# A two-layer trunk on one core: the first MLP with eight plain block products, its activations kept in SBUF

## The chip, the core and the metric

The kernel runs on one core of a Trainium2 chip. The metric is the device time of one execution in microseconds (us). The kernel before takes 2790.23 us, the median of three runs from 2789.31 to 2793.01 us.

The engines are named as the profile names them: PE is TensorE (matmuls), PEld its weight loads, DVE is VectorE, ACT is ScalarE, POOL is GpSimd, SP is SyncE, which here only issues DMAs.

## What is computed

The reference is a trunk of two layers over a sequence of 1024 tokens, 1024 channels wide. Layer 0 mixes tokens by retention, layer 1 by an S5 state-space layer. Each mixer is followed by an MLP with a causal convolution of width 3 on its gate. Every sub-layer is normed, and shifted, scaled and gated by the conditioning vector:

```python
def conv_ffn(h, w_up, conv_w, conv_b, w_down):
    val, gate = jnp.split(h @ w_up, 2, axis=-1)          # 1024 -> 2 x 2816
    gate = lax.conv_general_dilated(gate, conv_w, ...) + conv_b   # depthwise, 3 taps
    return (jax.nn.silu(gate) * val) @ w_down            # 2816 -> 1024

for i in range(DEPTH):                                   # 0: retention, 1: S5
    h = rms_norm(x) * (1.0 + sc1) + sh1
    x = x + g1 * mixer(h)
    h = rms_norm(x) * (1.0 + sc2) + sh2
    x = x + g2 * conv_ffn(h, ...)
return rms_norm(x) * final_norm_g
```

All of it is float32. The changed part is `conv_ffn` of layer 0.

## The kernel before

**Products.** Channels lie on the 128 partitions, tokens on the free axis, in two halves of 512 tokens (`hf`), which is one PSUM bank. A float32 product is made from split operands: each operand is a high part and a low part, and `mm3` issues three matmuls for each 128 x 128 weight block (high x high, high x low, low x high), at lines 765 to 767. A weight tile of 128 x 1024 is loaded raw (`wr`), and split by ScalarE (`whi`) and VectorE (`wlo`) into a ring of five. The class `Stream` (`W`) holds all weights of the program in one list, loads up to three raw tiles ahead, and splits the next one when the code asks for it (`get`) or passes a call of `pump`. The order of instructions is simply the order in which the Python code records them: each engine runs its instructions in that order and waits by semaphores.

**The MLP before.** `ffn` serves both layers. For one tile `ff` of 128 of the 2816 channels it makes gate and value of all tokens, a product of a 2 x 2 block matrix (gate and value by the two halves of the input channels) with another (the input halves by the token halves), from seven block products (`pair`) in place of eight. Each block product is 4 x 3 matmuls. Three things come with it: sums of weight blocks, made by GpSimd (`add_up`); sums of blocks of the normed activations, made once (`steps_s`, tiles `hs`); and sums of results: a bank gets one product, VectorE adds it into `u` or `E`, and then the same bank takes a second product on top (`b1`, `b3` and `b4` in `pair`). The convolved, gated result goes to DRAM (`store`, `ff_d`), since the slots of SBUF are full, and is read back and split for the down projection (`f_load`, `f_split`, tiles `fr`, `fh`, `fl`). Also x itself is stored before the MLP and read back for the down projection (`x_in`). The down projection runs over six groups of three or four tiles, after all up products.

**The background job.** While the first MLP runs, `s5_weights` makes the matrices of the S5 layer: 8 tiles with two rounds each, so 16 rounds. It is a Python generator. The MLP's code calls `bg` at fixed places, and each call records the job's next step; a bare `yield` ends a step, and `yield True` ends it and the call. A round is: products of table entries on GpSimd (`outer`), four transposes on TensorE (line 1392), angles and sines on GpSimd, VectorE and ScalarE, a second set of products, and four or eight small matmuls on TensorE (line 1414, the kernel products). After a tile's second round a small result goes to DRAM and comes back by eight loads (line 1431) in another layout, ScalarE reorders it (line 1439), and it is stored (`t_d`). The next tile starts behind that.

**Lead-ins.** Norms run in steps as well: `nrm.step` records the next one between groups of matmuls. `steps` makes the normed activations as pairs `hh`, `hl` for plain products (retention and S5 layers); `steps_s` makes the block sums for `pair`.

Of the kernel before, what the change touches and what calls it, by code (L numbers as in the profile page):

```python
# [18 lines left out]
P = 128  # L19
T = 1024  # L20
# [61 lines left out]
def trunk_kernel(ctx: ExitStack, tc: tile.TileContext, x, c, pos, ada_w, ada_b, ret_w_in, ret_w_out,  # L82
# [50 lines left out]
    def hsl(h):  # L133
        return slice(h * HW, (h + 1) * HW)
# [8 lines left out]
    def weight_list():  # L143
# [22 lines left out]
        yield from ffn_list(1)  # L166

    LEADS = 5
    GROUPS = ((0, 4), (4, 8), (8, 12), (12, 15), (15, 18), (18, 22))
# [3 lines left out]
    def ffn_list(l):  # L173
        wu, wd = ffn_w_up[l], ffn_w_down[l]
        for ff in range(LEADS):
            yield ("uv", l, ff), cols8(wu, ff * P), 8
        for ff in range(NFF):
            yield ("up", l, ff), (cols8(wu, FF + ff * P), cols8(wu, ff * P)), Q5 if ff < LEADS else Q7
        for ff in range(NFF):
            yield ("dn", l, ff), wd[ff * P:(ff + 1) * P, :].rearrange("p (o n) -> p o n", o=1), 1  # L180

    class Stream:
# [121 lines left out]
        def extra(self, i):  # L304
            key = self.items[i][0]
            return key[0] == "dn" and (key[2] % 8 > 4 and key[2] < GROUPS[-1][0] or key[2] in (1, 2))

# [1034 lines left out]
    def s5_weights():  # L1342
# [13 lines left out]
        nxt = load(0)  # L1356
        for _ in range(5):
            yield
        for j in range(8):
# [5 lines left out]
            for hf in range(2):  # L1365
# [67 lines left out]
            yield True  # L1433
            yield True
            yield True
            yield True
            yield True
            yield True
# [3 lines left out]
            yield True  # L1442
            yield True
        drop(sev)
# [121 lines left out]
    for b in range(1, HEADS):  # L1566
# [30 lines left out]
    ff_d = [tc.dram_tile((NFF, P, T), F32, name=f"ff{l}_d") for l in range(2)]  # L1597

    def ffn(l, finish, SB, behind=None):
        nonlocal xs  # L1600
        f_d = ff_d[l]
        e = t_p.tile([P, 1280], F32, tag="tA", name="E")
# [338 lines left out]

    ffn(0, finish0, SB, s5_weights())

# [356 lines left out]
```

## Time and profile before

| what | us |
|---|---|
| median of three runs | 2790.23 |
| the profiled execution | 2790.11 |
| its span, first to last instruction | 2788.3 |
| TensorE busy | 2628.9 |
| VectorE busy | 1763.3 |
| GpSimd busy | 1055.6 |
| ScalarE busy | 932.5 |

The span is one execution, as the hardware profiler saw it. A matmul of 512 columns is shown with a length of 0.39 us, while the next starts 0.227 us after it: matmuls overlap, so the busy time of TensorE is a union, and its pitch has to be read from starts. The stages of the program lie in the span like this, by the first matmul that reads a stage's tiles: retention up to 917 us; first MLP 917 to 1715 us, the down projection's matmuls from 1446 us; S5 layer with its GLU from 1715 to 2067 us; second MLP from 2067 us, its down projection from 2522 us.

### The profile page before, as it was taken

Reading aid. Unit: us, or ns where it says so; the run is one execution under the profiler, and the core shown is the slowest. Engines: PE = TensorE matmul, PEld = TensorE weight load, DVE = VectorE, ACT = ScalarE, POOL = GpSimd, SP = SyncE. Lnnn points to the kernel's source line nnn. Section 1 sums busy time; section 2 is a strip of 40 time slices with the busy share of each in tenths; the row PEclk is TensorE's granted clock in tenths of the full one; section 3 lists DMA queues with packets and bytes.
Section 4 is the critical chain, followed back from the end, with each engine's and each line's share of the span. In section 5 each row is a group of like instructions: output and inputs, shape, how many; then the busy total and the mean of one; then the engine's idle time right before and its main releaser. Section 6 shows DMA issues by size and latency. Waiting matters only on the chain.

```text
span 2788.3 us, 33464 instructions
## 1 busy us (share of the span) xinstructions
PE 2628.9 (94%) x12777; PEld 2199.2 (79%) x12777; DVE 1763.3 (63%) x2347; ACT 932.5 (33%) x1486; POOL 1055.6 (38%) x817
## 2 busy tenths in 40 slices
PE   6999999999999888999989999999998999999998
PEld 5798888888888676777777877888876788888887
DVE  8664664746765787777776654674248876666454
ACT  5332131221322634444433323322144444343112
POOL 5455676765101544655523333221124422310004
PEclk7999999999999999999999999999999999999999
DMA  7644344343532223333345433795221322225211
GB/s 241 169 129 137 121 135 145 117 158 94 168 115 69 91 93 106 119 108 119 113 176 183 137 127 129 248 301 184 75 83 61 106 83 84 83 86 207 101 53 61
DMA packets 319756, 356.59 MB, mean 128 GB/s; under 512 B 39372, under 2 KB 261100, under 8 KB 319596
## 3 DMA queue, kind: packets, MB, share of 16 engines
q1 hardware_dynamic: 278316, 276.17, 31.7%
q10 hardware_dynamic: 41280, 78.28, 7.6%
q8 instruction: 101, 1.65, 0.2%
q14 instruction: 59, 0.48, 0.1%
HBM read 266.64 MB, written 86.15 MB: 127 GB/s over the span
## 4 chain that ended last, share of the span: by engine, by line
PE 64%; DVE 18%; ACT 6%; issue 4%; DMA 4%; POOL 2%; SPq 0%; ACTq 0%; DVEq 0%; POOLq 0%
PE bk L765 20%; PE bk L767 19%; PE bk L766 19%; DVE t L1639 1%; DVE t L1638 1%; DVE whi L335 1%; DVE E L1210 1%; DVE wlo L335 1%; PE bk L1077 1%; PE bk L1075 1%; PE bk L1076 1%; DVE t L1210 1%; DVE sev L1396 1%; POOL ar L128 1%; DMA U<-u_d 1%
## 5 line engine op out<-in xcount | busy, mean ns | idle before, releaser
L765 PE MATMUL bk<-hs,whi 128*128 128x512 f32 x656 | 268.4, 409 | 44.7 <-DVE E L1210 41.2
L1473 DVE SCALAR_TENSOR_TENSOR x<-bk,mods,x 128x512 f32<-128x512 f32 x224 | 184.6, 832 | 192.5 <-PE bk L767 192.4
L766 PE MATMUL bk<-hs,whi 128*128 128x512 f32 x656 | 265.5, 405 | 6.4 <-DVE hs L657 4.3
L322 DVE TENSOR_TENSOR wlo<-wr,whi 128x1024 fp32r<-128x1024 f32 x126 | 179.7, 1430 | 138.4 <-ACT whi L321 138.4
L765 PE MATMUL bk<-hh,whi 128*128 128x512 f32 x640 | 255.7, 400 | 8.3 <-DVE x L1473 4.1
L767 PE MATMUL bk<-hs,wlo 128*128 128x512 f32 x656 | 260.2, 397 | 0.0
L766 PE MATMUL bk<-hl,whi 128*128 128x512 f32 x640 | 253.4, 396 | 3.0 <-POOL hl L128 1.7
L765 PE MATMUL bk<-hs,wlo 128*128 128x512 f32 x576 | 229.4, 398 | 26.0 <-DVE E L1210 26.0
L767 PE MATMUL bk<-hh,wlo 128*128 128x512 f32 x640 | 252.4, 394 | 0.2 <-DVE wlo L322 0.2
L767 PE MATMUL bk<-hs,whi 128*128 128x512 f32 x576 | 231.0, 401 | 0.0
L766 PE MATMUL bk<-hs,wlo 128*128 128x512 f32 x576 | 227.1, 394 | 0.0
L321 ACT ACTIVATE whi<-wr 128x1024 fp32r<-128x1024 f32 x126 | 131.5, 1056 | 284.6 <-PE bk L766 226.1
L765 PEld LDWEIGHTS bk<-hs,whi 128*128 128x128 f32 x656 | 128.7, 196 | 78.2 <-issue 28.1
L765 PE MATMUL bk<-fh,whi 128*128 128x512 f32 (+1 forms) x480 | 183.2, 382 | 5.3 <-ACT nat L2229 3.7
L767 PE MATMUL bk<-fh,wlo 128*128 128x512 f32 (+1 forms) x480 | 181.0, 377 | 0.0
L766 PE MATMUL bk<-fl,whi 128*128 128x512 f32 (+1 forms) x480 | 180.8, 377 | 0.0
L457 POOL TENSOR_TENSOR aacc<-aacc,ar 128x1024 f32<-128x1024 f32 x70 | 172.4, 2463 | 5.8
L128 POOL TENSOR_TENSOR nacc<-nacc,ar 128x512 f32<-128x512 f32 x36 | 46.6, 1294 | 322.1 <-ACT ar L575 321.9
L766 PEld LDWEIGHTS bk<-hs,whi 128*128 128x128 f32 x656 | 129.4, 197 | 34.8 <-DVE hs L657 5.0
L765 PEld LDWEIGHTS bk<-hs,wlo 128*128 128x128 f32 x576 | 110.2, 191 | 53.9 <-ACT wlo L334 12.5
L765 PEld LDWEIGHTS bk<-hh,whi 128*128 128x128 f32 x640 | 122.3, 191 | 35.4 <-ACT hh L611 4.5
L128 POOL TENSOR_TENSOR ar<-sp 128x512 f32<-128x512 f32 (+1 forms) x64 | 83.2, 1314 | 175.8 <-ACT sev L1402 81.8
(375 smaller groups left out, 6706.1 us busy)
## 6 DMA issues: line engine op xcount, KB each, us to landing
ar<-in_ada_w SPq DMA_DIRECT2D x80, 512.0 KB, 4.4
wr<-in_ffn_w_up SPq DMA_DIRECT2D x74, 512.0 KB, 3.8
wr<-in_ret_w_in SPq DMA_DIRECT2D x48, 512.0 KB, 3.8
ff_d<-t ACTq DMA_DIRECT2D x44, 512.0 KB, 2.8
wr<-in_ffn_w_down SPq DMA_DIRECT2D x44, 512.0 KB, 4.2
fr<-ff_d SPq DMA_DIRECT2D x44, 512.0 KB, 5.8
x_d<-x ACTq DMA_DIRECT2D x24, 512.0 KB, 3.1
x<-x_d SPq DMA_DIRECT2D x24, 512.0 KB, 7.2
```

Of the source, the lines that this page charges most:

```text
L128: GP.tensor_tensor(out=out, in0=in0, in1=in1, op=op)
L321: A.activation(out=hi, in_=r, func=AF.Copy)
L322: low = lambda: V.tensor_tensor(out=lo, in0=r, in1=f(hi), op=ALU.subtract)
L335: V.tensor_tensor(out=lo, in0=src, in1=f(hi), op=ALU.subtract)
L457: eng.tensor_tensor(out=acc, in0=acc, in1=raw, op=ALU.add)
L765: PE.matmul(bk, lhsT=lh, rhs=rh, start=first, stop=False, skip_group_check=skip)
L766: PE.matmul(bk, lhsT=lh, rhs=rl, start=False, stop=False, skip_group_check=skip)
L767: PE.matmul(bk, lhsT=ll, rhs=rh, start=False, stop=last, skip_group_check=skip)
L1075: PE.matmul(o, lhsT=hh, rhs=wh[:, k % 4, :], start=(k == 0), stop=False)
L1076: PE.matmul(o, lhsT=hh, rhs=wl[:, k % 4, :], start=False, stop=False)
L1210: V.tensor_tensor(out=o, in0=a, in1=b, op=op)
L1473: V.scalar_tensor_tensor(out=dst, in0=bk, scalar=g, in1=src, op0=ALU.mult, op1=ALU.add)
```

## The change

The first MLP gets a function of its own, `ffn_plain`; the second still calls `ffn`. In `ffn_plain` gate and value of a tile are plain products over the eight blocks of 128 input channels, for each half of the tokens: 24 matmuls into one bank, which is read once. ScalarE copies the gate to a tile `E` (now two of them, in turn), VectorE convolves it and multiplies it by the value's bank, and ScalarE and VectorE split the result at once into `fh` and `fl`, which stay in SBUF. The loop goes over 11 blocks of two tiles: up products of block b + 1, then the down projection of block b, added to x in its place; the last two blocks' down projection is `finish0`, as before with four tiles. The weight list is put in that order. x is neither stored before the MLP nor read back. The background job gets other places for its steps: one in the middle of each up product (`mid=bg`, after the fifth block), one behind it, and one after each m of the down projection; its own `yield`s are changed with it.

```diff
-        yield from ffn_list(0)
+        yield from plain_list(0)
...
+    def plain_list(l):
+        wu, wd = ffn_w_up[l], ffn_w_down[l]
+        for b in range(NB + 1):
+            if b < NB:
+                for ff in (2 * b, 2 * b + 1):
+                    yield ("ug", l, ff), cols8(wu, FF + ff * P), 8
+                    yield ("uv", l, ff), cols8(wu, ff * P), 8
...
+            for ff in dn:
+                yield ("dn", l, ff), wd[ff * P:(ff + 1) * P, :].rearrange("p (o n) -> p o n", o=1), 1
...
                 outer(8, O_RR, O_RI, O_Y1, O_Y2, True)
+                yield
+                yield
...
-                yield True
-                yield True
-                yield True
+                yield
                 bk = bank(6)
...
                 outer(9, O_AR, O_AI, O_Q1, O_Q2, False)
-                yield True
-                yield True
-                yield True
+                yield
+                yield
+                yield
...
-            SB = Blocks()
+            hT = []
...
-                    if hf:
-                        A.dma_start(out=x_d[m], in_=xs[m])
...
-                nrm.start_s(hf, xs, 0, 3, SB, 6, 7)
+                nrm.start(hf, xs, 0, 3, hT, 6, 7)
...
+    def ffn_plain(l, finish):
+        UB = DB = RA
...
+        def up_mm(w, hf):
+            bk = UB()
+            gemm(bk, w, hT, hf, sel=chalf, mid=bg)
+            return bk
+
+        def gate_out(bk, ff, hf):
+            e = E[ff % 2]
+            b3 = as_sel(bk, chalf)
+            A.activation(out=e[:, 2:10, hf * 64:(hf + 1) * 64], in_=b3, func=AF.Copy)
+            n = 64 - hf
+            A.activation(out=e[:, 0:2, hf * 64 + 1:hf * 64 + 1 + n], in_=b3[:, 6:8, 0:n], func=AF.Copy)
+
+        def val_out(bk, ff, hf):
...
+            V.tensor_scalar(out=a3, in0=e[:, 2:10, cs], scalar1=w2_, scalar2=None, op0=ALU.mult)
+            V.scalar_tensor_tensor(out=a3, in0=e[:, 1:9, cs], scalar=w1_, in1=a3, op0=ALU.mult, op1=ALU.add)
+            V.scalar_tensor_tensor(out=a3, in0=e[:, 0:8, cs], scalar=w0_, in1=a3, op0=ALU.mult, op1=ALU.add)
+            A.activation(out=s_, in_=a, func=AF.Silu, bias=cb)
+            V.tensor_tensor(out=s_, in0=s_, in1=bk, op=ALU.mult)
...
+            A.activation(out=hi[:, hsl(hf)], in_=s_, func=AF.Copy)
+            V.tensor_tensor(out=lo[:, hsl(hf)], in0=s_, in1=f(hi[:, hsl(hf)]), op=ALU.subtract)
+
+        def up(b):
+            for ff in (2 * b, 2 * b + 1):
+                wg = W.get(("ug", l, ff))
+                for hf in range(2):
+                    gate_out(up_mm(wg, hf), ff, hf)
+                    tick()
+                wv = W.get(("uv", l, ff))
+                for hf in range(2):
+                    val_out(up_mm(wv, hf), ff, hf)
+                    tick()
+
+        def lead():
...
+            for hf in range(2):
+                for grp in ((0, 1, 2, 3),) if hf == 0 else ((0, 1), (2, 3)):
+                    bks = [UB() for _ in grp]
...
+                    gemm_group(bks, [ws[i] for i in grp], hT, hf, chalf, step)
...
+        lead()
+        for b in range(NB - 2):
+            up(b + 1)
+            ffs = (2 * b, 2 * b + 1)
+            ws = W.get(("dn", l, ffs[0]), 2)
+            for m in range(8):
+                for hf in range(2):
+                    bk = down_mm(ws, ffs, m, hf)
+                    v = chalf(xs[m], hf)
+                    xadd(v, as_sel(bk, chalf), mod(l, 5, m), v)
+                tick()
+            for ff in ffs:
+                drop(*acts.pop(ff))
+        up(NB - 1)
+        bg_drain()
...
-    ffn(0, finish0, SB, s5_weights())
+    bgq.append(s5_weights())
+    ffn_plain(0, finish0)
```

The order of the instructions shows it on VectorE, at the end of a tile's products. Before, in the middle of a `pair`: `tu` is the running sum u, `bk` a bank, `E` the gate to be convolved, `t_7741` its convolution, and the rows of line 335 split weight blocks, among them sums (`sq`).

```order
L1210 TENSOR_TENSOR tu<-tu,bk 128x512
L335 TENSOR_TENSOR whi<-wr,whi 128x512
L1210 TENSOR_TENSOR E<-tu,bk 128x8x64
L335 TENSOR_TENSOR wlo<-wr,wlo 128x512
L1210 TENSOR_TENSOR E<-E,bk 128x8x64
L335 TENSOR_TENSOR whi<-wr,whi 128x512
L1210 TENSOR_TENSOR E<-tu,bk 128x8x64
L1638 SCALAR_TENSOR_TENSOR t_7741<-E,prm,t_7741 128x512
```

Now, from the last value half of a block into the down projection: `t_7740` is the convolution, `t_7741` its silu and then the product with the value's bank, `fl` the low part of the activation, and line 1486 (1473 before) adds a down product to x.

```order
L1638 TENSOR_SCALAR t_7740<-E,prm 128x512
L1639 SCALAR_TENSOR_TENSOR t_7740<-E,prm,t_7740 128x512
L1640 SCALAR_TENSOR_TENSOR t_7740<-E,prm,t_7740 128x512
L1642 TENSOR_TENSOR t_7741<-t_7741,bk 128x512
L1647 TENSOR_TENSOR fl<-t_7741,fh 128x512
L1486 SCALAR_TENSOR_TENSOR x_6527<-bk,mods,x_6527 128x8x64 x2
L339 TENSOR_TENSOR wlo<-wr,whi 128x1024
L1486 SCALAR_TENSOR_TENSOR x_6566<-bk,mods,x_6566 128x8x64 x2
```

The four reads of banks that build u and E are gone, and the additions to x stand directly behind a tile's activation.

On GpSimd, before, inside one round of the background job: `ar` and `sev` are its tiles, `wr`, `wrx` and `sq` the sums of weight blocks.

```order
L128 TENSOR_TENSOR ar<-sp 128x576 x2
L128 TENSOR_TENSOR ar<-ar 128x576
L128 TENSOR_TENSOR wr<-wr,sq 128x512
L128 TENSOR_TENSOR ar<-ar,db 16x2x16 x2
L128 TENSOR_TENSOR ar<-sp 128x4x8x16 x2
L128 TENSOR_TENSOR ar<-ar 128x512
L128 TENSOR_TENSOR sev<-sp,cst 128x512
L1385 TENSOR_SCALAR ar<-sev 128x512
L1386 TENSOR_SCALAR ar<-ar 128x512
L128 TENSOR_TENSOR sq<-wrx 128x512
```

Now, at the same place of a round (lines 1403 and 1404 are 1385 and 1386 before):

```order
L128 TENSOR_TENSOR ar<-sp 128x576 x2
L128 TENSOR_TENSOR ar<-ar 128x576
L128 TENSOR_TENSOR ar<-ar,db 16x2x16 x2
L128 TENSOR_TENSOR ar<-sp 128x4x8x16 x2
L128 TENSOR_TENSOR ar<-ar 128x512
L128 TENSOR_TENSOR sev<-sp,cst 128x512
L1403 TENSOR_SCALAR ar<-sev 128x512
L1404 TENSOR_SCALAR ar<-ar 128x512
```

The sums of weight blocks have left GpSimd's queue; the background job has it to itself. In TensorE's order, some 72 matmuls of the MLP now stand between the transposes of a round and its kernel product, some 48 between that and the second round's transposes, and 108 to 111 between a tile's last kernel product and the next tile's first transposes. From the S5 layer on, all engines have the instructions of before in the order of before.

## Rows read from the trace of the kernel before

**Rows 1.** The page: span, and busy time of each engine.

```profile
span 2788.3 us, 33464 instructions
PE 2628.9 (94%) x12777; PEld 2199.2 (79%) x12777; DVE 1763.3 (63%) x2347; ACT 932.5 (33%) x1486; POOL 1055.6 (38%) x817
```

**Rows 2.** By stretch, first MLP cut in two: length, busy per engine, clock, DMA share, GB/s.

```profile
917.00:1477.00 560.00, 493.84 (x2092) 395.48 (x2092) 425.86 (x505) 251.23 (x425) 280.96 (x221) 0.94 0.35 115
1477.00:1715.00 238.00, 231.19 (x1038) 187.99 (x1037) 136.11 (x158) 77.18 (x92) 87.29 (x81) 0.99 0.40 139
```

**Rows 3.** TensorE's waits, 917 to 1715 us: in total, times, longest.

```profile
PE bk L765 <- DVE E L1210: 50.4, 15, 9.8
PE bk L1414 <- POOL ar L128: 12.5, 6, 3.1
PE bk L1392 <- POOL ar L128: 4.0, 2, 3.3
PE bk L766 <- POOL E L1604: 2.0, 1, 2.0
...
```

**Rows 4.** In order of time, TensorE: start, duration, line, operation, tiles.

```profile
1559.73 0.39 PE L767 MATMUL bk<-fh,wlo 128*128 128x512 f32 x1
...
1563.13 0.39 PE L767 MATMUL bk<-fh,wlo 128*128 128x512 f32 x1
...
1736.63 0.39 PE L767 MATMUL bk<-hh,wlo 128*128 128x512 f32 x1
...
1738.89 0.39 PE L765 MATMUL bk<-hh,whi 128*128 128x512 f32 x1
```

**Rows 5.** Groups by line, TensorE, 917 to 1715 us: count, busy, mean ns, idle before.

```profile
L1414 PE MATMUL bk<-ar,sp 128*16 128x128 f32 x128 | 17.6, 283 | 12.5 <-POOL ar L128 12.5
L1392 PE MATMUL bk<-cst,ar 128*128 128x128 f32 x64 | 9.9, 279 | 4.0 <-POOL ar L128 4.0
```

**Rows 6.** TensorE in order of time, and the stretch 1089 to 1099 us.

```profile
1093.63 0.77 PE L765 MATMUL bk<-hs,whi 128*128 128x512 f32 x1 [9.82 <-DVE E L1210]
...
1089.00:1099.00 10.00, 5.37 (x12) 3.84 (x12) 6.97 (x9) 4.41 (x8) 3.34 (x2) 0.50 0.21 83
```

**Rows 7.** Groups by line, VectorE, 917 to 1715 us.

```profile
L1473 DVE SCALAR_TENSOR_TENSOR x<-bk,mods,x 128x512 f32<-128x512 f32 x96 | 70.9, 753 | 66.0 <-PE bk L767 65.9
L335 DVE TENSOR_TENSOR whi<-wr,whi 128x512 fp32r<-128x512 f32 x48 | 45.7, 953 | 27.4 <-ACT whi L334 27.4
L1638 DVE SCALAR_TENSOR_TENSOR t<-E,prm,t 128x512 f32<-128x512 f32 x44 | 45.5, 1034 | 16.4 <-ACT E L1628 16.4
L1639 DVE SCALAR_TENSOR_TENSOR t<-E,prm,t 128x512 f32<-128x512 f32 x44 | 42.2, 959 | 1.6
...
L322 DVE TENSOR_TENSOR wlo<-wr,whi 128x1024 fp32r<-128x1024 f32 x16 | 21.6, 1354 | 3.1 <-ACT whi L321 3.1
...
L798 DVE TENSOR_SCALAR sev<-sev 128x512 f32<-128x512 f32 x16 | 8.6, 539 | 0.5
```

**Rows 8.** TensorE in order of time, lead-in of the S5 layer.

```profile
1722.77 0.77 PE L765 MATMUL bk<-hh,whi 128*128 128x512 f32 x1 [4.08 <-DVE x L1473]
```

**Rows 9.** One passage of the background job: TensorE, SyncE's queue, ScalarE, TensorE.

```profile
1594.17 1.05 PE L1414 MATMUL bk<-ar,sp 128*16 128x128 f32 x8
...
1600.05 5.04 SPq L1431 DMA_DIRECT2D ar<-ks_d  x8
...
1613.40 2.22 ACT L1439 ACTIVATE ar<-ar 128x1024 f32<-128x1024 f32 x1
...
1621.25 0.89 PE L1392 MATMUL bk<-cst,ar 128*128 128x128 f32 x4 [3.33 <-POOL ar L128]
```

**Rows 10.** VectorE and GpSimd in order of time, 1169 to 1174 us.

```profile
1169.77 1.66 DVE L1639 SCALAR_TENSOR_TENSOR t<-E,prm,t 128x512 f32<-128x512 f32 x1
...
1173.16 0.75 DVE L1639 SCALAR_TENSOR_TENSOR t<-E,prm,t 128x512 f32<-128x512 f32 x1
...
1169.24 1.64 POOL L128 TENSOR_TENSOR sq<-sq,wr 128x512 f32<-128x512 f32 x1
```

More of the change, by code (lines that the diff above doesn't have):

```diff
@@ L180, in ffn_list @@
             yield ("dn", l, ff), wd[ff * P:(ff + 1) * P, :].rearrange("p (o n) -> p o n", o=1), 1
+    def plain_list(l):
[5 more added lines that the diff above has]
+                    yield ("uv", l, ff), cols8(wu, ff * P), 8
+            if b == NB:
+                dn = range(2 * NB - 4, 2 * NB)
+            elif 0 < b < NB - 1:
+                dn = range(2 * b - 2, 2 * b)
+            else:
+                dn = ()
+            for ff in dn:
+                yield ("dn", l, ff), wd[ff * P:(ff + 1) * P, :].rearrange("p (o n) -> p o n", o=1), 1
     class Stream:
@@ L305, in extra @@
             key = self.items[i][0]
-            return key[0] == "dn" and (key[2] % 8 > 4 and key[2] < GROUPS[-1][0] or key[2] in (1, 2))
+            return key[:2] == ("dn", 1) and (key[2] % 8 > 4 and key[2] < GROUPS[-1][0] or key[2] in (1, 2))
         def split(self, later=None):
@@ L1356, in s5_weights @@
         nxt = load(0)
-        for _ in range(5):
-            yield
+        yield
         for j in range(8):
@@ L1432, in s5_weights @@
                              in_=ks_d[j * 8:(j + 1) * 8, :, P - GI * t:2 * P - GI * t].rearrange("g i w -> i g w"))
[L1433 to L1438, printed above, removed]
+            yield
+            yield
+            yield
+            yield
             A.activation(out=tb.rearrange("p (g j t) -> p g t j", g=8, t=8),
@@ L1591, in trunk_kernel, with step, down_mm, down_group @@
                         nrm.behind(m)
-                nrm.start_s(hf, xs, 0, 3, SB, 6, 7)
+                nrm.start(hf, xs, 0, 3, hT, 6, 7)
     for a_, b_ in act:
         drop(a_, b_)
-    ff_d = [tc.dram_tile((NFF, P, T), F32, name=f"ff{l}_d") for l in range(2)]
+    def ffn_plain(l, finish):
+        UB = DB = RA
+        E = []
+        for tag in ("tA", "tD"):
+            e = t_p.tile([P, 1280], F32, tag=tag, name="E")
+            e3 = e.rearrange("p (t c) -> p t c", c=P)
+            GP.memset(e3[:, 0:2, 0:1], 0.0)
+            E.append(e3)
+        t1 = t_p.tile([P, 2, HW], F32, tag="tB", name="t1")
+        t2 = t_p.tile([P, 2, HW], F32, tag="tC", name="t2")
+        acts = {}
+        def up_mm(w, hf):
[9 more added lines that the diff above has]
+        def val_out(bk, ff, hf):
+            w0_, w1_, w2_, cb = convp(l, ff)
+            e = E[ff % 2]
+            cs = slice(hf * 64, (hf + 1) * 64)
+            a, s_ = t1[:, hf, :], t2[:, hf, :]
+            a3 = as_sel(a, chalf)
+            V.tensor_scalar(out=a3, in0=e[:, 2:10, cs], scalar1=w2_, scalar2=None, op0=ALU.mult)
[3 more added lines that the diff above has]
+            V.tensor_tensor(out=s_, in0=s_, in1=bk, op=ALU.mult)
+            if ff not in acts:
+                acts[ff] = (take(F32R, "fh"), take(F32R, "fl"))
+            hi, lo = acts[ff]
+            A.activation(out=hi[:, hsl(hf)], in_=s_, func=AF.Copy)
[11 more added lines that the diff above has]
+        def lead():
+            ws, late = [], {}
+            for i in range(4):
+                ws.append(W.get(("uv" if i % 2 else "ug", l, i // 2), more=(i > 0)))
+                W.pump()
+            for hf in range(2):
+                for grp in ((0, 1, 2, 3),) if hf == 0 else ((0, 1), (2, 3)):
+                    bks = [UB() for _ in grp]
+                    def step(k):
+                        if hf == 0:
+                            nrm.lead(k)
+                        else:
+                            nrm.step()
+                            if k in late:
+                                late.pop(k)()
+                    gemm_group(bks, [ws[i] for i in grp], hT, hf, chalf, step)
+                    for i, bk in zip(grp, bks):
+                        run = partial(val_out if i % 2 else gate_out, bk, i // 2, hf)
+                        if hf:
+                            run()
+                            W.done()
+                            tick()
+                        else:
+                            late[(0, 4, 1, 6)[i]] = run
+        def down_mm(ws, ffs, m, hf):
+            bk = DB()
+            n = len(ffs)
+            for i, ff in enumerate(ffs):
+                wh, wl = ws[i]
+                mm3(bk, wh[:, 0, m * P:(m + 1) * P], wl[:, 0, m * P:(m + 1) * P],
+                    acts[ff][0][:, hsl(hf)], acts[ff][1][:, hsl(hf)], i == 0, i == n - 1)
+            return bk
+        lead()
[8 more added lines that the diff above has]
+                    xadd(v, as_sel(bk, chalf), mod(l, 5, m), v)
+                tick()
+            for ff in ffs:
+                drop(*acts.pop(ff))
+        up(NB - 1)
+        bg_drain()
+        for p_, q_ in hT:
+            drop(p_, q_)
+        ffs = tuple(range(NFF - 4, NFF))
+        ws = W.get(("dn", l, ffs[0]), 4)
+        def down_group(ms, hf):
+            bks = {m: DB() for m in ms}
+            for i, ff in enumerate(ffs):
+                wh, wl = ws[i]
+                for m in ms:
+                    mm3(bks[m], wh[:, 0, m * P:(m + 1) * P], wl[:, 0, m * P:(m + 1) * P],
+                        acts[ff][0][:, hsl(hf)], acts[ff][1][:, hsl(hf)], i == 0, i == 3)
+                if i < 1:
+                    nrm.step(1)
+                if i:
+                    W.done()
+                    W.pump()
+                if i == 3:
+                    nrm.step(2)
+            W.done()
+            return bks
+        def down_part(m, c0, nc):
+            bk = DB()
+            sel = lambda t: t[:, hsl(c0 // 64)].rearrange("p (t c) -> p t c", t=8)[:, :, c0 % 64:c0 % 64 + nc]
+            o = bk[:, 0:8 * nc].rearrange("p (t c) -> p t c", t=8)
+            for i, ff in enumerate(ffs):
+                wh, wl = ws[i]
+                mm3(o, wh[:, 0, m * P:(m + 1) * P], wl[:, 0, m * P:(m + 1) * P],
+                    sel(acts[ff][0]), sel(acts[ff][1]), i == 0, i == 3)
+            return o
+        finish(down_part, down_group)
+        for ff in ffs:
+            drop(*acts.pop(ff))
```

8 lines of the change are left out of this document (5 added, 3 removed).

## The prediction

> **What bounds the kernel now.** I read the page's busy times first, then the stretch of the first MLP cut in two, then TensorE's waits in it, and last the rows from which prices come. TensorE is busy for 2628.9 of 2788.3 us [rows 1]; no other engine comes over 63%. So the time is TensorE's instructions at their pitch, plus the stretches in which it stands still or runs at half clock. The profiled execution took 2790.1 us, 1.8 us more than its span, and the median of the runs is 2790.2 us; the sum below is made against 2790.1.
>
> The first MLP runs from 917 to 1715 us. In its first 560 us (the block products, and the first groups of the down projection) TensorE is busy for 493.8 us and the granted clock averages 0.94; in the other 238 us, all of it down projection, 231.2 us and 0.99 [rows 2]. The waits tell why the two differ: 50.4 us in 15 places stand before a product whose releaser is a VectorE addition into E, line 1210 [rows 3]. That is the chain of the seven products: a bank may take its second product only once VectorE has read the first. Another 12.5 and 4.0 us stand before the small matmuls of the background job that prepares the S5 layer's weights, and wait for GpSimd; what is left is 5.7 us, most of it in the lead-in of the MLP. All nine rows of that view sum to 72.6 us; the four largest are shown. A long wait costs twice: after 9.8 us of idling TensorE works at a granted clock of 0.50, the 1.2 GHz level, for these 10 us [rows 6]. The share of clock lost is 0.06 x 560 + 0.01 x 238 = 36 us.
>
> A check that nothing large is missed: matmuls start every 0.2267 us (15 steps from 1559.73 to 1563.13) in the down projection, and 10 steps from 1736.63 to 1738.89 give 0.226 us for a product that reads half of the normed activations with stride, as the new code will [rows 4]. The MLP has 22 x 7 x 4 x 3 = 1848 up and 22 x 16 x 3 = 1056 down matmuls: 2904 x 0.2267 = 658.3 us. The background's small matmuls take 17.6 + 9.9 = 27.5 us [rows 5]. 658.3 + 27.5 + 72.6 + 36 = 794.4 us of 798.
>
> **The change part by part.**
>
> *TensorE's work.* A gate and value tile now takes eight plain block products in place of seven: 22 x 2 x 2 x 8 x 3 = 2112 matmuls, 264 more. 264 x 0.2267 = +59.8 us, all on the path, since TensorE is what the kernel waits for. The Trainium skill (TensorE: Matmul & The Clock Gate, Back-to-back issue gap) gives 131 ns for such a matmul in a sustained stream, and about 216 ns for one by itself; 264 of them would be 35 or 57 us. The rows have 227 ns in every dense stretch, so the trace disagrees with the first and is 5% above the second.
>
> *The waits of the seven products.* In the new code a bank is filled by 24 matmuls in a row and read once afterwards; no product waits for VectorE between them. Six banks rotate: a bank comes back six products, 6 x 24 x 0.2267 = 33 us, later. VectorE's work on a value half is one scalar multiply, two multiply-adds, the multiply by the bank and the low part. The first is new; I bound it by 0.54 us (line 798) and 0.96 us (line 1639); with 1.03 + 0.96, 0.75 (an instruction that reads a bank, line 1473) and 0.95 us the half costs 4.2 to 4.7 us, where two products take 10.9 us [rows 7]. So the 50.4 us go. What is late next is the background job, below.
>
> *VectorE as a whole.* 44 halves x 4.4 = 194, 66 weight tiles x 1.354 = 89, 160 additions to x at 0.753 = 120 us: 403 us, and about 16 x 5 x 1.0 = 80 us for the background, in 750 us of TensorE work. Before it was 425.9 + 136.1 = 562 us [rows 2, 7]. It has become lighter, mainly as the splitting of block sums and the split on the way back from DRAM are gone. GpSimd loses all its block sums. This counts for VectorE too: one and the same multiply-add takes 1.66 us when it starts during a GpSimd addition and 0.75 us when none runs [rows 10]. The Trainium skill (SBUF — State Buffer, Who interferes with whom) has this as a lock: a VectorE instruction with two SBUF inputs and a GpSimd instruction that reads SBUF exclude each other. The trace agrees.
>
> *DRAM traffic.* 22 stores of activations, 22 loads, and the 8 stores and 8 loads of x around the MLP go. TensorE waits for none of them in [rows 3], so I cost them at nothing; SyncE's queue keeps the weight loads and the background's alone. The up projection's weights are the same bytes, and one weight tile lasts two products, 10.9 us; with three raw and five split buffers a late load is hidden, and would cost its own lateness if not.
>
> *The background job.* It is still 16 rounds with 64 + 128 small matmuls: 27.5 us, unchanged. Its steps are now spaced by half a product, 2.7 us, and in TensorE's order some 72 matmuls (16.3 us) stand between the transposes and the kernel product of a round. GpSimd's three additions there, at about 1.64 us each [rows 10], take 5 us, so most of the 12.5 us should go. The tight place is from one tile's last kernel product to the next tile's first transposes: 108 matmuls or a few more, 24.5 us. Before, one such passage began at 1594.2 us and the transposes came at 1621.25 us after 3.33 us of waiting, 27.1 us in all; in between stand the eight loads from 1600.05 us (5.04 us of issuing) and ScalarE's copy at 1613.40 us [rows 9]. A load of stored activations that is gone now ran between the two. So seven passages wait 0 to 2.6 us each: 0 to 18 us. For all of the background the bounds are 0 and today's 16.5 us plus the lost clock. I take 6 us.
>
> *The lead-in.* The MLP now begins as the S5 layer does, with four products side by side while the norm's second half is made. That lead-in has one wait of 4.08 us [rows 8]; the present one of the MLP has most of the 5.7 us above. Bounds 0 and 8; I take 4 us.
>
> *Lost clock.* 36 us were lost for 72.6 us of waits, 0.5 us for each. 10 us of waits left make 15 us with the clock.
>
> *The sum.* The MLP: 798 - 72.6 - 36 + 59.8 + 15 = 764 us, a gain of 33.8 us: 2790.1 - 33.8 = 2756 us. From the S5 layer on, the engines' instructions are the same as before in the same order, so I cost the rest at nothing.
>
> **The rivals.**
>
> *No wait is left.* Every wait in [rows 3] goes: 72.6 + 36 - 59.8 = 48.8 us gained, 2741 us. For it: the second half of the MLP, with its plain groups, waits for nothing but the background. Against: seven passages with next to no slack. If a matmul could go at the page's 131 ns it would be 2716 us; nothing in [rows 4] speaks for it, and I give it one in a hundred, inside this case.
>
> *The background keeps its waits.* The 16.5 us stay, with 8 us of clock, and the lead-in doubles its 6 us: gain 48.8 - 24.7 - 12 = 12 us, 2778 us. For it: the same chain through ScalarE, GpSimd and DRAM, with fewer steps of patience written between its parts. Against: GpSimd does nothing else now.
>
> *VectorE holds up the down groups (slower).* A down group has 16 half products of 1.36 us, 21.8 us in all, and comes after every second tile, while VectorE still finishes a value half. It has 16 x 0.753 = 12.0 us of additions, up to three weight tiles (4.1 us), a half round of the background (5 us) and 1.7 us left over: 22.8 us at worst, with six banks (8 us) to lean on. If GpSimd's additions stretch these as in [rows 10], it passes 25.7 us, and the 3.9 us more in each of ten groups eat the gain; from there on it is slower. At 28 us the groups cost 62 us with the lost clock neglected: about 2818 us. Against: the second half of the MLP runs such groups with the same job beside them, VectorE 57% busy (136.1 of 238 us), and TensorE waits for no addition to x there [rows 2, 3].
>
> *Nothing gained.* Waits of 33 us (with half as much clock) remain in places that I don't see: 2790 us.
>
> **How the numbers follow.** The forecast, 2756 us with a range of its own of 2745 to 2771, has 0.66. No wait left: 0.11. The background's waits: 0.11. Nothing gained: 0.05. VectorE holds up the groups: 0.07. What a measurement of this kernel can tell from no change is about 0.2%, 5.6 us, so faster has 0.66 + 0.11 + 0.11 = 0.88, same 0.05, slower 0.07. The range from 2740 to 2780 us takes in the first three cases but for their ends and leaves out some 15 in 100.
>
> **What would show it.** TensorE's matmuls of the first MLP go to 2112 + 1056 at 0.227 us; no wait for VectorE's additions into E is left in the first MLP; the MLP lasts about 764 us; the granted clock there is over 0.97; waits before the transposes (line 1392 before) number up to seven and stay under 3 us; the second MLP keeps its own. I am wrong if TensorE waits for additions to x in the down groups, if single waits of over 3 us at the value products keep the clock at half, or if the rest of the span changes by over 5 us.

## The result and the profile after

The changed kernel takes 2743.3 us (median of 4 runs, 2740.0 to 2746.8), the kernel before 2790.1 on the same chip: a ratio of 0.9831 with a 95% interval of 0.9814 to 0.9848, 47 us faster. The forecast was 2756 us, with a range from 2740 to 2780.

First the page of the changed kernel, which answers to [rows 1]:

```profile
span 2740.5 us, 33365 instructions
PE 2652.0 (97%) x13041; PEld 2228.7 (81%) x13041; DVE 1651.2 (60%) x2248; ACT 856.9 (31%) x1348; POOL 908.8 (33%) x724
```

TensorE has 264 instructions more (13041 for 12777) and is busy for 23 us longer, and still the span is 47.8 us shorter: the rest was standing still and half clock. The first MLP, cut at the same 1477 us as in [rows 2] (stretch, length, busy time of PE, PEld, DVE, ACT, POOL with counts, clock, DMA share, GB/s):

```profile
917.00:1477.00 560.00, 551.24 (x2497) 448.88 (x2496) 350.74 (x432) 194.90 (x290) 184.57 (x178) 1.00 0.29 92
1477.00:1672.00 195.00, 195.00 (x876) 160.94 (x876) 97.61 (x127) 55.20 (x84) 32.10 (x30) 1.00 0.22 72
```

TensorE is busy for 551 of the first 560 us, where it was 494, at a clock of 1.00, where it was 0.94. Its waits in the same stretch, which answer to [rows 3] (what was waited for; us in total, times, longest):

```profile
PE bk L782 <- DVE t L1642: 3.5, 2, 2.5
PE bk L1408 <- POOL ar L128: 2.0, 3, 1.0
PE bk L783 <- DVE hl L637: 1.6, 1, 1.6
PE bk L783 <- POOL hl L128: 0.8, 1, 0.8
PE bk L1430 <- POOL ar L128: 0.7, 1, 0.7
```

8.6 us are left of 72.6, and no row names E. (Lines 1408 and 1430 are 1392 and 1414 of before.) The table shows where the span went. A stage runs from its first matmul to the next stage's first; "gaps" is the sum of TensorE's idle times over 0.3 us, "clock" half of the time at a granted clock of 0.50.

| stage | before | gaps, clock | after | gaps, clock |
|---|---|---|---|---|
| ahead of the first MLP | 918.2 | | 917.8 | |
| first MLP | 797.1 | 72.4, 37.5 | 759.5 | 8.6, 0 |
| S5 layer | 351.7 | 8.8, 3.4 | 349.4 | 6.4, 1.7 |
| second MLP, up | 455.1 | 22.7, 10.2 | 454.5 | 22.8, 10.2 |
| its down projection, final norm | 266.2 | 7.7, 1.4 | 259.4 | 2.2, 1.7 |

The first MLP gained 37.6 us. Another 9.1 came from the S5 layer and the last stage, which compute what they did before. The last stage's waits show it best. Before:

```profile
PE bk L765 <- ACT nat L2229: 3.7, 3, 1.4
PE bk L2223 <- DVE xn L1473: 1.6, 2, 0.8
PE bk L765 <- DVE nat L2232: 1.5, 2, 1.0
PE bk L2214 <- DVE facc L2252: 0.9, 1, 0.9
```

And after, the same view:

```profile
PE bk L2364 <- DVE facc L2402: 0.9, 1, 0.9
PE bk L2373 <- DVE xn L1486: 0.7, 1, 0.7
PE bk L782 <- DVE nat L2382: 0.5, 1, 0.5
```

A product of the down projection no longer waits for ScalarE to finish `nat`, the transposed output. These two have nothing to do with each other but a PSUM bank.

### The profile page after: what moved, and what is told of

It is laid out like the page before. It is cut to its first block, busy times and chain, and to the rows that moved or that the text cites. A ratio compares the mean times of both kernels' runs of the same rounds, so it can differ in the third digit from the quotient of the medians.

```text
span 2740.5 us, 33365 instructions
## 1 busy us (share of the span) xinstructions
PE 2652.0 (97%) x13041; PEld 2228.7 (81%) x13041; DVE 1651.2 (60%) x2248; ACT 856.9 (31%) x1348; POOL 908.8 (33%) x724
## 4 chain that ended last, share of the span: by engine, by line
PE 75%; DVE 13%; ACT 4%; DMA 3%; issue 2%; POOL 2%; SPq 0%; ACTq 0%; DVEq 0%; POOLq 0%
PE bk L782 23%; PE bk L784 23%; PE bk L783 23%; PE bk L1094 1%; PE bk L1092 1%; PE bk L1093 1%; DMA W<-w_d 1%; DVE wlo L339 1%; POOL ar L128 1%; ACT whi L338 1%; DVE stf L1167 1%; PE bk L2150 1%; DVE bacc L476 1%; PE bk L1188 1%; DVE gve L1154 0%
## 5 line engine op out<-in xcount | busy, mean ns | idle before, releaser
L782 PE MATMUL bk<-hh,whi 128*128 128x512 f32 x1344 | 530.7, 395 | 7.3 <-DVE t L1642 2.5
L783 PE MATMUL bk<-hl,whi 128*128 128x512 f32 x1344 | 526.7, 392 | 5.5 <-POOL hl L128 2.6
L784 PE MATMUL bk<-hh,wlo 128*128 128x512 f32 x1344 | 526.0, 391 | 0.3 <-DVE wlo L339 0.3
L339 DVE TENSOR_TENSOR wlo<-wr,whi 128x1024 fp32r<-128x1024 f32 x173 | 239.3, 1385 | 261.0 <-ACT whi L338 260.3
L782 PEld LDWEIGHTS bk<-hh,whi 128*128 128x128 f32 x1344 | 254.2, 189 | 63.2 <-DVE t L1642 2.9
L783 PEld LDWEIGHTS bk<-hl,whi 128*128 128x128 f32 x1344 | 253.8, 189 | 60.4 <-POOL hl L128 5.7
L784 PEld LDWEIGHTS bk<-hh,wlo 128*128 128x128 f32 x1344 | 253.8, 189 | 53.9 <-DVE wlo L339 0.7
L1092 PE MATMUL bk<-whi,hh 128*128 128x256 f32 x512 | 147.2, 288 | 0.0
L1094 PE MATMUL bk<-whi,hl 128*128 128x256 f32 x512 | 144.8, 283 | 0.0
L1093 PE MATMUL bk<-wlo,hh 128*128 128x256 f32 x512 | 144.8, 283 | 0.0
L782 PE MATMUL bk<-hs,whi 128*128 128x512 f32 x328 | 130.6, 398 | 7.3 <-DVE E L1227 6.7
L783 PE MATMUL bk<-hs,whi 128*128 128x512 f32 x328 | 130.4, 398 | 3.3 <-DVE hs L674 3.3
```

The source lines that it names most:

```text
L339: low = lambda: V.tensor_tensor(out=lo, in0=r, in1=f(hi), op=ALU.subtract)
L782: PE.matmul(bk, lhsT=lh, rhs=rh, start=first, stop=False, skip_group_check=skip)
L783: PE.matmul(bk, lhsT=lh, rhs=rl, start=False, stop=False, skip_group_check=skip)
L784: PE.matmul(bk, lhsT=ll, rhs=rh, start=False, stop=last, skip_group_check=skip)
L1092: PE.matmul(o, lhsT=hh, rhs=wh[:, k % 4, :], start=(k == 0), stop=False)
L1093: PE.matmul(o, lhsT=hh, rhs=wl[:, k % 4, :], start=False, stop=False)
```

## The experiments

The kernel before was run again beside each group of kernels (medians from 2791.9 to 2795.8 us), so gains are taken from ratios, times 2790.1 us. Each ratio is known to between 0.001 and 0.002, 2.5 to 5.5 us. "MLP" is the first MLP in the profiled execution, as in the table above; four of the executions below have the changed kernel's MLP as it is (after, a_phase, a_plain2, a_q5), and agree on it within 0.8 us. b_nobgv, a_k7 and a_k7old leave work out.

| kernel | edit | ratio (95%) | us by ratio | MLP |
|---|---|---|---|---|
| after | | 0.9831 (0.9814 to 0.9848) | 2742.9 | 759.5 |
| b_phase | before, other banks in two places | 0.9949 (0.9931 to 0.9968) | 2775.9 | 798.4 |
| a_phase | after, old banks in the last stage | 0.9865 (0.9845 to 0.9884) | 2752.4 | 759.0 |
| b_nobgv | before, no VectorE work in the job | 0.9838 (0.9823 to 0.9852) | 2744.9 | 754.2 |
| b_swap | before, A12 ahead of A22 | 0.9971 (0.9958 to 0.9984) | 2782.0 | 783.8 |
| b_newbg | before, the job's new pauses | 1.0186 (1.0172 to 1.0201) | 2842.0 | 846.6 |
| a_oldbg | after, the job's old pauses | 0.9808 (0.9792 to 0.9825) | 2736.5 | 756.3 |
| a_k7 | after, 240 matmuls fewer | 0.9766 (0.9747 to 0.9785) | 2724.8 | 740.1 |
| a_k7old | the same, old pauses | 0.9657 (0.9643 to 0.9671) | 2694.4 | 711.1 |
| a_db2 | after, two banks in the down groups | 0.9989 (0.9980 to 0.9997) | 2787.0 | 804.9 |
| a_st | after, 44 stores more | 0.9852 (0.9836 to 0.9869) | 2748.8 | 764.7 |
| a_plain2 | after, second MLP plain too | 0.9917 (0.9903 to 0.9932) | 2766.9 | 758.8 |
| a_q5 | after, other order in five tiles | 0.9837 (0.9822 to 0.9851) | 2744.6 | 759.6 |

### Where the 9 us outside the MLP came from

The banks 0 to 5 go round in the shared rotation `RA`. The new MLP takes its banks from it and leaves it two places further on; the old one had a list of its own.

> The kernel before, with another order of PSUM banks in two places and nothing else: the four products that open the S5 layer take their banks in the rotation of the down projection ahead of them, and the last stage's transposes start on banks 0, 1, 2, 3 and not on 4, 5, 0, 1. Theory (the 9 us that the changed kernel saves outside the first MLP are bank order, since the new MLP leaves the shared rotation two places further on): the 4.08 us wait in the lead-in of S5 and the six waits of the last stage go, 2.3 + 6.8 us, so 2790 becomes 2781 us. Rival (they come from less DRAM traffic or lighter engines): no change, 2790 us.

```diff
     ffn(0, finish0, SB, s5_weights())
+    RA.ids = [2, 3, 5, 0, 4, 1]
...
+    RA.ids, RA.i = [2, 3, 4, 5, 0, 1], 4
     ffn(1, finish1, SB)
```

> The changed kernel, with the rotation of PSUM banks moved on by four places ahead of the second MLP, so that the last stage's transposes take the same banks as in the kernel before. Theory (bank order): the waits of fh products for nat come back in the last stage and it takes 266 us in place of 259.4, so 2743.3 becomes 2750 us. Rival (lighter traffic or engines): no change, 2743 us.

```diff
+    RA.i += 4
     ffn(1, finish1, SB)
```

The S5 layer and the last stage of b_phase, the kernel before with other banks:

```profile
1721.00:2069.30 348.30, 341.77 (x1827) 293.87 (x1825) 175.08 (x268) 94.06 (x141) 65.75 (x56) 1.00 0.59 187
2523.70:2783.20 259.50, 251.06 (x1233) 211.87 (x1231) 133.86 (x166) 55.08 (x71) 30.00 (x42) 0.99 0.29 104
```

The last stage of a_phase, the changed kernel with the old banks there:

```profile
2486.40:2752.60 266.20, 252.23 (x1233) 211.96 (x1231) 133.79 (x166) 54.95 (x71) 30.01 (x42) 0.99 0.28 101
```

The old kernel's last stage falls from 266.2 to 259.5 us and its S5 layer from 351.7 to 348.3; the changed kernel's last stage goes back to 266.2. The times by ratio move by -14.2 and +9.5 us, each within its uncertainty of what the stages show. Over all traces, the last stage takes 266.2 us in the five with the old banks there and 259.4 to 261.4 in the eight with the others; the S5 layer takes 351.7 to 358.2 us in the four with its old banks and 347.0 to 350.9 with others, but for the 352.9 of a_st. So the 9 us are bank order, and not traffic or lighter engines: b_phase has both as before. Worked out from the rotations: in the old order the down product after two groups of transposes was given the bank of one of the two, which ScalarE or VectorE was still copying out; and the first four products of the S5 lead-in had bank 4 among theirs, which one of the last two additions to x had yet to read ([rows 8], the 4.08 us). The S5 layer gains less than these 4.08 us, as later waits for loads differ from run to run.

### What the waits for E were

> The kernel before, with two of the seven products of a gate and value tile exchanged in both MLPs: A12 is computed ahead of A22, so that two products and not one stand between the first writing of a bank and its second. The work is the same. Theory (the 50.4 us are the chain of the seven products: a second product comes one product, 2.72 us, after the first, and VectorE is late by up to 9.8 us now and then): each wait of a tile with A12 shrinks by up to 2.72 us. The three waits in the tiles of the lead-in, which have no A12, stay (13.1 us); the other twelve go from 36 to about 15 us, and with half of that as lost clock the gain is some 30 us, 2760 us. Rival (VectorE is short of time as a whole while the background job runs, so a wait that goes here comes back at the next read): under 5 us, 2785 to 2790 us.

```diff
-    Q7 = ("A11", "S2", "S3", "S1", "A22", "A12", "S4")
+    Q7 = ("A11", "S2", "S3", "S1", "A12", "A22", "S4")
```

(and the calls in `pair` in that order). TensorE's waits in the first MLP of b_swap:

```profile
PE bk L765 <- DVE E L1210: 32.2, 12, 5.9
PE bk L1414 <- POOL ar L128: 15.6, 7, 4.4
PE bk L1392 <- POOL ar L128: 6.0, 3, 3.0
PE bk L765 <- ACT tu L1664: 5.5, 2, 5.2
```

Both theories got a part. E falls from 50.4 to 32.2 us, as with a product more of patience, but 5.1 us of it come back at the small matmuls and 5.5 at ScalarE's copy. The MLP gains 13.3 of the 30 us; 6.5 are lost again in the S5 layer, where the 4.08 us wait stays and later ones for loads are longer. By the ratio 8 us are gained, between the two expectations.

> The kernel before with VectorE's part of the background job left out (the six instructions that reduce the angles in each of 16 half rounds; the two sines become copies), so its output differs. What TensorE, GpSimd and the DMA queues do for the job stays. Theory A (the 50.4 us of waits for E belong to the chain of the seven products, whatever else VectorE does): over 40 of the 50.4 us stay, 2780 us or more. Theory B (they are VectorE's queue: the job's instructions, stretched by GpSimd's additions beside them, stand ahead of the reading of a bank): the three waits of the lead-in tiles stay (13.1 us), the other 36 fall under 15, and with half of that as clock the time falls by some 30 us to 2760.

```diff
-                for c_ in (TWO_PI_1, TWO_PI_2):
-                    V.scalar_tensor_tensor(out=ev1, in0=kq, scalar=-c_, ...)
...
-                V.scalar_tensor_tensor(out=kq, in0=ev1, scalar=-1.0, in1=ev1, ...)
-                A.activation(out=ev0, in_=kq, func=AF.Sin, scale=-1.0, bias=hpi)
-                A.activation(out=ev1, in_=ev1, func=AF.Sin, scale=sgn)
+                A.activation(out=ev0, in_=kq, func=AF.Copy)
+                A.activation(out=ev1, in_=ev1, func=AF.Copy)
```

TensorE's waits in its first MLP:

```profile
PE bk L765 <- DVE E L1210: 29.7, 11, 6.3
PE bk L1409 <- POOL ar L128: 4.6, 2, 2.8
PE bk L1392 <- POOL ar L128: 3.4, 2, 3.2
```

Theory B in the main: the waits of the lead-in tiles stay (5.9 + 4.1 + 2.6 us), the others fall from 37.3 to 17.0 us, where it gave 15, and the small matmuls' from 16.5 to 8.0. The MLP takes 754.2 us, with seven products and less time than the changed kernel's.

The second MLP of the kernel before has the same products and the same sums of weight blocks, and no job. So it shows what the chain does by itself. TensorE's waits for E in the kernel before, in the first MLP up to 1070 us (its first six tiles) and from there on; in b_nobgv from 1070 us on; and in the second MLP before, 2067 to 2522 us:

```profile
PE bk L765 <- DVE E L1210: 14.8, 5, 5.9
PE bk L765 <- DVE E L1210: 35.6, 10, 9.8
PE bk L765 <- DVE E L1210: 14.8, 6, 6.3
PE bk L765 <- DVE E L1210: 16.8, 6, 5.9
```

Of the six waits in the second MLP, five (16.2 us) stand in the same first six tiles. So some 15 of the 50.4 us come with or without a job. The other 35.6 come only beside it: 20.8 of them go with the job's VectorE instructions, and 14.8 stay with the rest of the job, its GpSimd additions among it. No run takes those away, so what they do by themselves is open.

The longest wait of before shows VectorE's queue. TensorE issues a matmul at 1083.41 us and then none before 1093.63 ([rows 6]). VectorE, and below it GpSimd, in order of time (start, duration, line, operation, tiles), before:

```profile
1079.44 1.77 DVE L335 TENSOR_TENSOR whi<-wr,whi 128x512 fp32r<-128x512 f32 x1
1081.14 3.40 DVE L1396 SCALAR_TENSOR_TENSOR sev<-ar,sev 128x512 f32<-128x512 f32 x2
1084.58 0.69 DVE L1398 SCALAR_TENSOR_TENSOR sev<-ar,sev 128x512 f32<-128x512 f32 x1
...
1087.69 1.71 DVE L335 TENSOR_TENSOR wlo<-wr,wlo 128x512 fp32r<-128x512 f32 x1
...
1091.14 1.74 DVE L335 TENSOR_TENSOR wlo<-wrx,wlo 128x512 fp32r<-128x512 f32 x1
1092.81 0.67 DVE L1210 TENSOR_TENSOR E<-tu,bk 128x512 f32<-128x512 f32 x1
...
1080.62 1.74 POOL L128 TENSOR_TENSOR wrx<-wr,wrx 128x512 f32<-128x512 f32 x1
1082.32 1.67 POOL L128 TENSOR_TENSOR ar<-sp 128x576 f32<-128x576 f32 x1
```

The reading of the bank is the line at 1092.81, 0.67 us long. Ahead of it stand the job's angles (lines 1396 to 1400) and the low parts of weight blocks and their sums (line 335). The two instructions of line 1396 take 1.70 us each while GpSimd adds, and the one of line 1398 takes 0.69 when it has stopped. That is what [rows 10] show, again, and the change took GpSimd's block sums away as well; what this stretching costs by itself no run shows.

### The pauses of the job and the price of a matmul

> The kernel before with the background job's steps spaced as in the changed kernel (its new list of pauses), everything else as before. Theory (what helped the job was the longer run of plain products between its steps, not the new list): no gain, 2785 to 2795 us; if anything its own waits of 16.5 us grow, since the new list has fewer pauses. Rival (the new spacing itself is worth the 12 us): 2780 us or less.

> The changed kernel with the background job's old list of pauses. Theory (the waits went because plain products leave VectorE and GpSimd time, whatever the list): within 5 us of the changed kernel, 2743 to 2748. Rival (the passages that the new list spaces out come back as waits before the small matmuls): 10 us or more, 2753 us and up.

The edits exchange `s5_weights` between the two kernels. The list of pauses is in the change above, but for two parts: the five `yield` at the job's start became one, and between two tiles `yield True`, six times and then twice, became `yield`, four times and then once. In b_newbg TensorE waits for:

```profile
PE bk L765 <- DVE E L1210: 44.1, 11, 7.7
PE bk L1413 <- POOL ar L128: 29.5, 9, 8.6
PE bk L1391 <- POOL ar L128: 25.8, 7, 10.2
```

In the old MLP the new list costs 52 us: the waits at the small matmuls go from 16.5 to 55.3 us. Theory and rival both missed that: the first had 2785 to 2795 us, and said only that these waits might grow. In the new MLP the two lists cannot be told apart (2736.5 against 2742.9 us by overlapping intervals; an MLP of 756.3 and 759.5 us). So the list earned nothing; a_oldbg's time by ratio is even 6.4 us lower, where its theory allowed 5.

> The changed kernel with the last of the eight block rows left out of 80 of the 88 up products of the first MLP (all but those of its lead-in), so its output differs: 240 matmuls of 128 x 512 fewer. Theory (TensorE's pitch is the price, 0.2267 us each, and nothing else is near to binding): 54.4 us less, 2689 us. Rival (VectorE, the weight loads or the background job are close behind TensorE in the new MLP): waits appear and less than 40 us are gained, 2703 us or more. By the Trainium skill's 131 ns for a matmul in a stream (TensorE: Matmul & The Clock Gate) it would be 31 us, 2712 us.

```diff
-            gemm(bk, w, hT, hf, sel=chalf, mid=bg)
+            gemm(bk, w, hT, hf, sel=chalf, mid=bg, ks=range(7))
```

Neither 54 nor 31 us came but 18. TensorE's waits in its first MLP:

```profile
PE bk L1408 <- POOL ar L128: 14.7, 6, 4.5
PE bk L782 <- DVE t L1642: 6.9, 3, 3.7
PE bk L782 <- DVE x L1486: 4.2, 4, 2.2
PE bk L1430 <- POOL ar L128: 3.9, 5, 1.5
```

Six waits, 14.7 us in all, stand before transposes (line 1408), where the changed kernel has 2.0 us. Three of them (4.5, 2.1 and 2.5 us) end the job's passage from one tile to the next, and three (3.1, 1.1 and 1.5 us) stand between the two rounds of a tile: 24 matmuls in a product had just covered the job, and 21 don't. The next run put that to the test.

> The changed kernel with 240 up matmuls of the first MLP left out (the last of eight block rows in 80 of 88 products, so its output differs), and with the background job's old list of pauses. With the new list the same kernel took 2728 us and not the 2689 expected: 32 us of waits in the first MLP, 18.6 of them at the job's small matmuls. From a tile's last kernel product to the next tile's first transposes the new list has 9 pauses, with 21 matmuls each now about 21 us, and the old one 12, about 29 us; the chain of loads and copies between them took 23.8 us in the kernel before. Theory (the waits are this passage, and the list sets it): under 4 us at the transposes, and 2700 to 2708 us. Rival (VectorE or GpSimd is short of time in the shortened MLP, whatever the list): 15 us of waits or more at the small matmuls or behind VectorE, 2718 us or more.

Two figures in this text are wrong. The chain between two tiles did not take 23.8 us in the kernel before but the whole 27.1 of [rows 9], of which TensorE waited for 3.33. And a passage of a_k7 lasts 24.2 to 29.5 us, not 21: it still has 96 to 108 matmuls, since part of it lies in a down group, which a_k7 does not shorten.

Its waits:

```profile
PE bk L782 <- DVE t L1646: 5.3, 2, 2.8
PE bk L782 <- DVE x L1490: 2.5, 2, 1.9
PE bk L783 <- DVE hl L637: 1.5, 1, 1.5
```

No wait at the transposes is left; the passages from tile to tile now last 29.0 to 33.1 us. In this shortened MLP the list alone is worth 30 us, and the time is below the range expected. The same 240 matmuls are now worth 42 us by the ratios (0.9808 to 0.9657) and 45.2 in the MLP (756.3 to 711.1). With 5.9 us more of gaps and 1.7 of clock that makes 52.8 us, 0.220 us for each, close to the pitch of [rows 4]. The 131 ns that the Trainium skill gives for such a stream (TensorE: Matmul & The Clock Gate, Back-to-back issue gap) would make an estimate of 31 us for the 240; the runs don't have it.

### The banks, the stores, and the second MLP

> The changed kernel with two PSUM banks in turn, in place of six, for the half products of the nine down groups in the first MLP. A half product is 6 matmuls, 1.36 us, so a bank has to be read within that time of its last matmul. Theory (VectorE comes late by several microseconds at the start of a group, and the six banks carry this): 3 us or more in each group, 2770 us and up, with waits for x additions. Rival (VectorE has time to spare there, and the depth of banks is worth nothing): under 6 us, 2743 to 2749 us.

```diff
+        D2 = Rot([2, 3])
...
-                    bk = down_mm(ws, ffs, m, hf)
+                    bk = down_mm(ws, ffs, m, hf, D2)
```

Its waits in the first MLP:

```profile
PE bk L782 <- DVE x L1486: 24.0, 10, 6.3
PE bk L782 <- DVE t L1643: 9.2, 4, 5.5
```

It is 44 us slower than the changed kernel: in the MLP 29 us more of gaps and 15 of clock. VectorE comes up to 6.3 us late to a down group, mostly at its start; six banks of 1.36 us had hidden that.

> The changed kernel with 44 more stores, one for each half of an activation tile (128 x 512, 256 KB) to a DRAM buffer that nothing reads, issued by ScalarE: the stores that the change removed, and nothing of their loads. Theory (the traffic costs nothing, since no wait of TensorE ends on it): within 4 us of the changed kernel, 2739 to 2748. Rival (the stores delay the weight loads or ScalarE's issue enough to show): 8 us or more.

```diff
+    fx_d = tc.dram_tile((NFF, P, T), F32, name="fx_d")
...
             V.tensor_tensor(out=s_, in0=s_, in1=bk, op=ALU.mult)
+            A.dma_start(out=fx_d[ff][:, hsl(hf)], in_=s_)
```

Between the two theories: 5.9 us by the ratios, whose intervals overlap, and 5.2 us in the MLP, against 0.8 us between the four executions of the unchanged one. So stores that nothing waits for may not be quite free; one traced execution does not settle it.

> The changed kernel with its second MLP in the same plain form as the first: eight products for each tile and half, activations kept in SBUF, no store and reload of x around it. No background job runs there. Theory (what the plain form removed in the first MLP was mostly the job's meeting with the block sums on VectorE, so without the job it only costs its 264 matmuls): +59.8 us, less most of the 33 us of waits and lost clock in the second MLP's first 455 us: 2743 + 35 = 2778 us. Rival (the plain form is worth its gain by itself, through the shorter chain): 2743 us or less.

```diff
-        yield from ffn_list(1)
+        yield from plain_list(1)
...
-    ffn(1, finish1, SB)
+    ffn_plain(1, finish1)
```

(and, as in the first MLP's change, the norm ahead of it makes plain pairs, and x is not stored.)

The rows go from the second MLP's first matmul to the end, first in the changed kernel and then in a_plain2:

```profile
2026.60:2740.50 713.90, 682.73 (x3097) 565.72 (x3095) 460.80 (x599) 254.69 (x422) 179.90 (x146) 0.98 0.27 93
```

```profile
2032.50:2769.70 737.20, 730.46 (x3361) 610.24 (x3359) 373.70 (x498) 177.69 (x285) 40.14 (x52) 1.00 0.15 48
```

All waits but one go, and it is still 23.3 us slower (24 by the ratios; 35 were expected): 264 matmuls, 59.8 us, less the 25.0 us of gaps and 11.9 of clock that the table has for these stages. Without the job beside them, seven products win.

> The changed kernel, where the first five tiles of the second MLP compute their five products in the order S3, S1, S2, A22, S4 in place of S2, S3, S1, A22, S4, with one more VectorE addition each. So two products stand between the first and the second writing of each bank, not one. In the changed kernel the five waits for E, 15.7 us, all lie in these tiles. Theory (they are late by one product, and VectorE has the time): under 5 us of them stay, and with half of the rest as clock the time falls by some 15 us to 2728. Rival (VectorE as a whole is behind in these tiles, so the wait moves to the next read): within 4 us of the changed kernel, 2739 to 2747.

```diff
-    Q5 = ("S2", "S3", "S1", "A22", "S4")
+    Q5 = ("S3", "S1", "S2", "A22", "S4")
```

(with `pair` in that order, and one more addition of `b2` into E for these tiles). Its waits in the up stage:

```profile
PE bk L782 <- DVE E L1227: 7.7, 5, 2.6
PE bk L783 <- POOL hs L128: 3.8, 4, 1.4
PE bk L783 <- DVE hs L674: 3.5, 2, 3.3
```

The rival holds: E halves from 15.7 us, more waits for the block sums of the activations (`hs`) appear, and the time is the same. (Of the five waits for E that the expectation puts into these tiles, the last, 1.8 us, stands in the sixth.) No version run here that does the whole work beats the changed kernel by more than the measurement can tell; a_oldbg comes lowest, with an interval that overlaps.

## Why the prediction was right, and where it was not

**TensorE's work, +59.8 us: right.** The trace has 2112 up and 1056 down matmuls. Their price is the pitch as long as the job is not in the way (a_k7old). In the kernel as it is, it is partly covered: without the eighth of a product the job would have waited instead (a_k7).

**The waits for E, -50.4 us: right in size, partly right in cause.** I put them down to the chain of the seven products. The chain exposes TensorE, and with no job beside it, in the second MLP, it costs 16.8 us, nearly all in the first six tiles. The other 35.6 us of the first MLP came with the job: 20.8 of them through its VectorE instructions (b_nobgv), and more patience alone moved the waits on (b_swap). How much of the remaining 14.8 is VectorE stretched by GpSimd's additions is not shown.

**What is left, 15 us: 8.6.** The job was put at 6 us and measured 2.7 (lines 1408 and 1430), in four waits of up to 1.0 us. The seven passages between tiles, put at 0 to 2.6 us each, wait twice, for 0.7 and 1.0 us. They last 25.5 to 26.8 us from the start of the kernel product; the 27.1 us that I compared count from there too, and my 24.5 only from its end, 1 us later. So the margin was thin, as a_k7 showed. The lead-in was put at 4 and has 4.9 of the other 5.9. Lost clock was put at 5 us more and is none: 0.5 us of clock for each microsecond of waiting, taken from long waits, did not hold for waits of 2.5 us and less. In part that is luck: in five of nine executions the longest of these waits did cost clock (last section). So the MLP lasts from 917 us to the S5 layer 760.2 us, and not 764.

**The rest of the span at nothing: wrong, by 9.1 us.** This is the step that failed. I argued that the instructions from the S5 layer on are the same in the same order. They are, but not on the same banks, and that made five waits of the last stage and one in the lead-in of S5 go (b_phase, a_phase). By my own test, a change of over 5 us in the rest of the span, that part was wrong; with the MLP's 3.8 us it makes the 13 us between forecast and result.

**DRAM traffic at nothing:** not settled; 5 us of gain may be in the stores (a_st), and no run brings back the loads.

**The rivals.** VectorE does come late to the down groups, as the slower case had it, and the six banks that I named against it are what keeps the time (a_db2: with two it would have been 44 us). The background's waits did not stay. "No wait is left" comes closer to the time with 2741 us, but by another sum: it had 48.8 us in the MLP, where 37.6 came.

## What to carry to other kernels

A Strassen-like scheme, as the seven products are, saves matmuls, but makes TensorE wait for the engine that reads its banks; price it by what else stands in that engine's queue: here it lost beside a background job and won by 23 us without one. A wait that is hidden by a margin of a microsecond is not gone: take away some of the work that covers it and it is back, as with the job's pauses. And where two stages share a rotation of banks, a change in one moves the other's banks: look who held each bank last before costing an unchanged stage at nothing.

## What the runs showed of the hardware

The same wait may or may not cost clock. In the lead-in of the first MLP the changed kernel waits for 2.51 us, and a_k7old for 2.54 us at the same place. The stretch of 11 us around it, first in the changed kernel, then in a_k7old:

```profile
957.00:968.00 11.00, 8.60 (x38) 7.13 (x39) 6.99 (x10) 4.31 (x7) 1.88 (x3) 1.00 0.01 1
```

```profile
961.00:972.00 11.00, 9.43 (x34) 7.66 (x35) 6.96 (x11) 4.30 (x7) 1.14 (x2) 0.84 0.01 1
```

The granted clock stays at 1.00 (2.4 GHz) in the one and averages 0.84 in the other, where it is 0.50 (1.2 GHz) for 3.4 us. Nine traced kernels have this wait in their first MLP, 2.51 to 2.54 us long. In four executions the clock stays (the changed kernel, a_phase, a_plain2, a_q5), and in five it falls for 3.4 us (a_oldbg, a_db2, a_k7, a_k7old, a_st), which is 1.7 us lost. So a wait of this size can be priced only with a spread.
